# Wide two-operand work moved off GpSimd, norm gains folded into the split as columns, delta-rule state updated for two heads at once

## The chip, the cores and the metric

The kernel runs on one core of a Trainium2 chip. The metric is device time in microseconds (us) of one execution; lower is better. Engines are called PE (TensorE, matrix products), PEld (its weight loads), DVE (VectorE), ACT (ScalarE), POOL (GpSimd) and SP (SyncE, which issues the DMAs).

## The reference, cut to what matters

Two blocks run one after the other on `x` (1 x 512 x 1024, float32). The first block has two layers, and each layer is a mixer followed by a feed-forward part. The mixer projects the normed input and feeds four groups of four heads: hgrn2, gated linear attention, MLA attention and a gated delta rule. Its output norms carry a gain per head channel:

```python
def hgrn2_mixer(...):
    o = rms_norm(o, norm_g) * jax.nn.sigmoid(heads(g, HA, DV_A))     # gla and gdn: silu
def chunk_gated_delta(...):                       # per chunk of 64 tokens
    v_new = u_ - w_ @ state
    o = (q_ * exp(b_)) @ state + a_ @ v_new
    state = exp(b_last) * state + (k_ * exp(b_last - b_)).T @ v_new
```

The second block has layer A (differential attention, whose output is normed with the gain `a_subln_2` over 128 channels, times 1 - lambda_init, times a silu gate) and layer B (stick-breaking attention). Both layers also attend to a memory.

## The kernel before, in words

Everything is float32. A matrix product is three float32r products: each operand is kept as a high and a low part (`split`, `mm3`), so every weight tile of 128 x 1024 that arrives by DMA (`wr`) is cast by ACT to the high part (`wh`) and a subtraction gives the low part (`wl`) in `wload`. That subtraction runs on DVE, or on POOL where the caller gives `eng=self.G`: this is so for the tiles that `setup` preloads (two) and for those that `out_proj` preloads for the stage to come (three ahead of each feed-forward part, two ahead of layer 1 of the first block, of layer A and of layer B), 14 in all.

The program is written as generators, but its order is not theirs: `Plan` records every operation with its tiles, and `simulate` lists them by a cost model (`cost`, with a price for each engine; POOL's tensor_tensor 0.15 + 2.1 ns per element, DVE's 0.07 + 1.04 ns per element) with the program's order as the priority. The instructions are then emitted in that order, and each engine executes its own in order. The model takes the engines as independent of one another apart from data and buffers. All instructions carry one helper's line (L328), so a group in the profile is known by its tiles: `p4w`, `p4p`, `p4h` are 128 x 1024 buffers, `p` 128 x 512 ones, `st` small columns, `bc` and `cols` constants, `psA`, `psS`, `psD` PSUM banks (3, 3 and 2).

A layer of the first block runs as: norm of four token tiles (`norm_tok`, whose root comes from POOL: `rstd`), transposes and splits into `h` (`trans_split`: ACT high, DVE low), projections merged with the heads' cores (`merge`), then `out_proj` with `residual_norm` for each token tile, and interleaved with it the next norm; then 22 steps of the feed-forward part, and its `out_proj`.

What the change touches in these stages: `gate_done` (activation of a gate, then its product with the norm's gain on POOL), `finish` and `to_mixT` (product of output and gate, of the norm, transposes, split), `gla_core` (`qk`, and `AT` from the diagonal), `gdn` (three 128 x 1024 products of a mask and a column vector, `gm` twice and `sq`; `v` times beta; `kbe`; the state update of the delta rule, four operations on 64 partitions x 64 for each of 7 chunk steps), `fm_to_tm` (transposes, evacuated by ACT), `gates` and `emit_y` in layer A, and the tables `prow` (rows that become columns of `cols`) and `pbc` (rows broadcast to 128 partitions, `bc`).

Of the kernel before, what the change touches and what calls it, by code (L numbers as in the profile page):

```python
# [15 lines left out]
ALU = mybir.AluOpType  # L16
# [18 lines left out]
def shape_constants():  # L35
# [36 lines left out]
    for k, v in c.items():  # L72
# [8 lines left out]

_ROWS = [("mq", 4), ("mkv", 2), ("lb", 4), ("bgk", 2), ("hc", 6), ("f0", 66), ("g0", 24), ("pad", 20),
         ("f1", 66), ("g1", 24), ("pad2", 38)]
_BCS = [("hg", 128), ("gg", 128), ("dg", 128), ("alog", 8), ("dtb", 8), ("sub", 128), ("g16", 32)]

# [13 lines left out]
def pack(I):  # L99

    f = lambda k: np.asarray(I[k], np.float32)
    z = lambda n: np.zeros((n, 128), np.float32)
    heads = [f("a_q_norm_2")[0], f("a_k_norm_2")[0], f("mem_q_norm_2")[0], f("mem_q_norm_2")[1],
             f("mem_k_norm_2")[0], f("mem_k_norm_2")[1]]
    rows = {"mq": f("mla_q_norm_g"), "mkv": f("mla_kv_norm_g"), "lb": f("hgrn_lb_logits"), "bgk": f("gla_b_gk"),
            "hc": np.stack([np.concatenate([h, h]) for h in heads]), "pad": z(20), "pad2": z(38),
            "f0": f("ffn_conv_w")[0], "f1": f("ffn_conv_w")[1], "g0": f("gdn_conv_w")[0], "g1": f("gdn_conv_w")[1]}
    prow = np.concatenate([rows[k].reshape(-1, 128) for k, _ in _ROWS])
    bcs = {"hg": f("hgrn_norm_g"), "gg": f("gla_norm_g"), "dg": f("gdn_norm_g"), "alog": f("gdn_a_log"),
           "dtb": f("gdn_dt_bias"), "sub": f("a_subln_2"),  # L110
           "g16": np.concatenate([heads[0][:16], heads[1][:16]])}
    pbc = np.concatenate([bcs[k].reshape(-1) for k, _ in _BCS])
    w = f("w_in")
    wsm = np.concatenate([w[:, :, OFF[k]:OFF[k] + n] for k, n in (("bc", 16), ("db", 8), ("ckr", 32))], axis=2)
    return {"consts": CONST_ARR, "neg": NEG_ARR, "prow": np.ascontiguousarray(prow),
            "pbc": np.ascontiguousarray(pbc),
            "plam": np.concatenate([f(f"a_lambda_{k}_2")[0] for k in ("q1", "k1", "q2", "k2")]), "wsm": np.ascontiguousarray(wsm)}
# [496 lines left out]
class Net:  # L614
# [334 lines left out]
    def setup(self):  # L949
# [13 lines left out]
        for t in (2, 3):  # L963
            self.preload(first[t - 2], eng=self.G)
            load(t)
# [5 lines left out]
    def setup1(self):  # L971
# [16 lines left out]
        b = lambda k, l, n: bc[:, BC_OFF[k] + l * n:BC_OFF[k] + (l + 1) * n]  # L988
        self.hg, self.gg, self.dg = ([b(k, l, 64) for l in range(2)] for k in ("hg", "gg", "dg"))
        self.alog, self.dtb = ([b(k, l, 4) for l in range(2)] for k in ("alog", "dtb"))  # L990
        self.sub8, self.g16 = b("sub", 0, 128), b("g16", 0, 32)
        self.w2 = self.cst([16, 2, 128], name="w2")
# [40 lines left out]

    def to_mixT(self, o, kt0, pst):

        for g in range(2):
            ps = self.ps(pst)
            for t in range(NT):
                self.tr(ps[:, t * 128:(t + 1) * 128], o[:, t, g * 128:(g + 1) * 128])
            mt = self.p4([128, 2, S], F32R)  # L1040
            self.split(mt[:, 0, :], mt[:, 1, :], ps)
            self.mixT[kt0 + g] = mt

    def finish(self, o, gate, kt0, pst):

        sq = self.p4()
        self.act(sq, o, AF.Square)
        ss = self.st([128, 16])
        self.rsum(ss, sq.rearrange("p (a d) -> p a d", d=64))
        yield lambda: gate.get("done")  # L1050
        r = self.rstd(ss, 64)
        self.mul(o, o, gate["gate"])
        yield self.when(r)
        ov = o.rearrange("p (a d) -> p a d", d=64)
        self.mul(ov, ov, r.unsqueeze(2).broadcast_to([128, 16, 64]))
        yield self.when(o)
        self.to_mixT(o.rearrange("p (t c) -> p t c", t=NT), kt0, pst)

# [8 lines left out]
    def gate_done(self, T, f, g):  # L1067

        self.act(T["gate"], T["gate"], f)
        gv = T["gate"].rearrange("p (a d) -> p a d", d=64)  # L1070
        self.mul(gv, gv, g.unsqueeze(1).broadcast_to([128, 16, 64]), self.G)
        T["done"] = True

    def gla_core(self, q, k, b, v, dk, scale, out):
# [46 lines left out]
        qk = big()  # L1121
        self.mul(qk, q, k, self.G)
        el = self.st([128, nc8])
# [32 lines left out]
        diag = self.K["lev"][:, 6 * 64:7 * 64].unsqueeze(1).broadcast_to([128, 16, 64])  # L1156
        self.mul(a3(AT), diag, dg.unsqueeze(2).broadcast_to([128, 16, 64]), self.G)
        yield self.when(E, Q)
# [359 lines left out]

    def fm_to_tm(self, src, dst):

        dv = dst.rearrange("p (t j c) -> p t j c", t=NT, j=2)
        for j in range(2):
            ps = self.ps("D")
            for t in range(NT):
                self.tr(ps[:, t * 128:(t + 1) * 128], src[:, j * S + t * 128:j * S + (t + 1) * 128])
            self.act(dv[:, :, j, :], ps.rearrange("p (t c) -> p t c", t=NT), AF.Copy)

# [8 lines left out]
    def gdn(self, l, qkv, T0):  # L1536
# [31 lines left out]
        ex = self.st([128, 64])  # L1568
        self.act(ex, ps[:, :64], AF.Exp)
        eb, er = ex[:, 0:16], ex[:, 16:32]  # L1570
# [18 lines left out]
        m4 = lambda key: K[key].unsqueeze(1).unsqueeze(1).broadcast_to([128, 2, 8, 64])  # L1589
        self.mul(v4(gm), m4("gt64"), sta(gf), self.G)  # L1590
        yield self.when(gm)
        for half in range(2):
# [3 lines left out]
            self.act(lm[:, s], ps, AF.Exp)  # L1596
        self.mul(v4(sq), m4("gt64"), sta(nbetaf), self.G)
        yield self.when(rk)
# [46 lines left out]

        self.mul(v4(gm), m4("le64"), sta(gf), self.G)
        self.mul(v3(q), v3(q), bc16(eb))
# [12 lines left out]
        v = self.p4()  # L1660
        self.fm_to_tm(vraw, v)
        self.mul(v3(v), v3(v), bc16(betaf), self.G)
        yield self.when(Nb)
# [51 lines left out]
        self.mul(sc, betaf, eb)  # L1715
        self.mul(v3(kbe), v3(k), bc16(sc), self.G)
        self.mul(v3(k), v3(k), bc16(er))
# [19 lines left out]
        for c in range(8):  # L1737
# [11 lines left out]
            for h in range(4):  # L1749
                self.mm(ps[hr(h), (h // 2) * 64:(h // 2) * 64 + 64], kd[prs(c), tslot(h, c)], vn[prs(c), slot(h, c)])  # L1750
            for h in range(4):
                e0 = 32 + (c % 2) * 16 + (c // 2) * 4 + h
                self.stt(Sa[hr(h), c + 1, h // 2, :], Sa[hr(h), c, h // 2, :], ex[hr(h), e0:e0 + 1],
                         ps[hr(h), (h // 2) * 64:(h // 2) * 64 + 64], ALU.mult, ALU.add)
            yield self.when(Sa)
# [67 lines left out]
    def out_proj(self, W, lhs, order, done, first, second, then):  # L1823
# [26 lines left out]
        for t in range(NT):  # L1850
# [4 lines left out]
            if t == NT - 1:  # L1855
                self.preload(*then, eng=self.G)
            done(t, [ps0[t], ps1[t]])
# [267 lines left out]
    def layer_a(self, steps):  # L2125
# [114 lines left out]
        def gates(g):  # L2240
# [5 lines left out]
            def last():  # L2246
                self.act(gate[g], gate[g], AF.Silu)
                gv = gate[g].rearrange("p t (h d) -> p (t h) d", d=128)
                self.mul(gv, gv, self.sub8.unsqueeze(1).broadcast_to([128, 8, 128]), self.G)

# [45 lines left out]
    def emit_y(self, y, tag):  # L2296
# [4 lines left out]
        o = self.p4([128, 2, S], F32R, tag)  # L2301
        self.split(o[:, 0, :], o[:, 1, :], ps)
        return o
# [216 lines left out]
```

## Time and profile before

| | |
|---|---|
| time, median of 3 runs | 2048.59 us (2046.83 to 2051.95) |
| the profiled execution's own time | 2043.82 us |
| its span, first to last instruction | 2042.0 us |
| busy: PE, DVE, ACT, POOL | 1963.9, 1265.9, 955.0, 356.8 us |
| mean granted TensorE clock | 0.989 |
| DMA | 191.88 MB, mean 94 GB/s |

The span falls into six stretches: mixer of layer 0 (0 to 365 us), its feed-forward part (365 to 733), mixer of layer 1 (733 to 1089), its feed-forward part (1089 to 1457), layer A (1457 to 1750) and layer B (1750 to 2042). A profile row of a timeline gives start, length, engine, operation, tiles and shape, and in brackets how long the engine had been idle before and what ended that. A granted clock of 1.00 is the 2.4 GHz level, 0.50 the 1.2 GHz level.

### The profile page before, as it was taken

To read this page: it belongs to the slowest core of one execution; us is meant where nothing else is said; L and a number is where in the kernel's file an instruction comes from. 1 tells how busy PE (TensorE), PEld (TensorE's weight loads), DVE (VectorE), ACT (ScalarE), POOL (GpSimd) and SP (SyncE) were. 2 spreads that over 40 slices of the span, in tenths; PEclk is the share of its full clock that TensorE was granted. 3 is DMA by queue.
4 is the path that set the end of the run, shared out by engine and by line. 5 is a ranking of instruction groups with operands and counts; after the bars stand their busy time and mean duration, and the time that the engine had idled before them with its cause. 6 is when DMAs were issued, how large, how long until landed. Compare 5 with 4: busy or idle time off the path is not lost.

```text
span 2042.0 us, 33217 instructions
## 1 busy us (share of the span) xinstructions
PE 1963.9 (96%) x13254; PEld 1663.4 (81%) x13254; DVE 1265.9 (62%) x2313; ACT 955.0 (47%) x1721; POOL 356.8 (17%) x403
## 2 busy tenths in 40 slices
PE   6999999999999999999999999999999999999999
PEld 5888778888888878787788888888899988888787
DVE  7697883644442266879836444422548886558796
ACT  5763363433332246633634333322446663457782
POOL 3312121100000023112203000000323331105131
PEclk9999999999999999999999999999999999999999
DMA  5321224433332433301344333325331213331121
GB/s 159 99 71 36 71 67 164 117 100 93 94 102 93 155 108 93 76 23 55 94 150 119 93 94 102 93 93 175 114 83 49 77 62 114 126 91 53 62 73 62
DMA packets 231305, 191.88 MB, mean 94 GB/s; under 512 B 22224, under 2 KB 201072, under 8 KB 231152
## 3 DMA queue, kind: packets, MB, share of 16 engines
q1 hardware_dynamic: 231152, 189.77, 30.4%
q8 instruction: 104, 1.70, 0.4%
q14 instruction: 49, 0.40, 0.1%
HBM read 174.54 MB, written 15.20 MB: 93 GB/s over the span
## 4 chain that ended last, share of the span: by engine, by line
PE 80%; DVE 11%; ACT 3%; issue 2%; POOL 2%; DMA 1%; SPq 1%; DVEq 0%; ACTq 0%; POOLq 0%
PE psA L328 59%; PE psS L328 12%; PE psD L328 9%; DVE p4w L328 7%; DVE wl L328 1%; POOL st L328 1%; DVE p L328 1%; DVE st L328 1%; ACT p4w L328 1%; DVE p4p L328 1%; SPq L328 1%; ACT wh L328 1%; DVE p4h L328 0%; DMA p4p<-in_x_dram 0%; ACT p L328 0%
## 5 line engine op out<-in xcount | busy, mean ns | idle before, releaser
L328 PE MATMUL psA<-p4h,wh 128*128 128x512 f32 (+1 forms) x2144 | 626.0, 376 | 4.0 <-ACT p4h L328 2.6
L328 DVE TENSOR_TENSOR wl<-wr,wh 128x1024 fp32r<-128x1024 f32 (+5 forms) x290 | 336.6, 1165 | 392.2 <-ACT wh L328 386.8
L328 ACT CAST wh<-wr 128x1024 fp32r<-128x1024 f32 (+6 forms) x304 | 299.0, 990 | 474.8 <-PE psA L328 283.8
L328 PEld LDWEIGHTS psA<-p4h,wh 128*128 128x128 f32 x2144 | 392.6, 190 | 83.2 <-ACT p4h L328 4.4
L328 PE MATMUL psA<-p4h,wl 128*128 128x512 f32 (+1 forms) x1072 | 403.2, 377 | 1.5 <-DVE wl L328 1.5
L328 PE MATMUL psA<-wh,p4h 128*128 128x256 f32 (+1 forms) x1792 | 353.0, 290 | 2.1 <-DVE p4h L328 1.7
L328 PEld LDWEIGHTS psA<-wh,p4h 128*128 128x128 f32 x1792 | 284.0, 190 | 6.6 <-DVE p4h L328 2.3
L328 PE MATMUL psA<-wl,p4h 128*128 128x256 f32 (+1 forms) x896 | 259.8, 290 | 0.0
L328 POOL TENSOR_SCALAR st<-st 128x1 f32<-128x1 f32 (+4 forms) x108 | 40.0, 370 | 1139.1 <-ACT p4w L328 781.4
L328 PEld LDWEIGHTS psA<-p4h,wl 128*128 128x128 f32 x1072 | 203.9, 190 | 35.5 <-DVE wl L328 1.7
L328 PEld LDWEIGHTS psA<-wl,p4h 128*128 128x128 f32 x896 | 170.5, 190 | 1.6
L328 PE MATMUL psA<-wh,p4w 128*128 128x512 f32 (+1 forms) x540 | 159.5, 368 | 0.0
L328 ACT ACTIVATE p<-p 128x512 f32<-128x512 f32 (+2 forms) x174 | 88.1, 526 | 107.1 <-DVE p L328 105.9
L328 POOL TENSOR_TENSOR st<-st,c 128x1 f32<-128x1 f32 (+4 forms) x106 | 113.9, 1077 | 7.5
L328 PEld LDWEIGHTS psA<-wh,p4w 128*128 128x128 f32 x540 | 96.5, 188 | 18.4 <-issue 0.7
L328 ACT ACTIVATE p4w<-psA 128x256 f32<-128x256 f32 (+5 forms) x138 | 61.6, 451 | 101.9 <-PE psA L328 100.9
L328 PE MATMUL psS<-p4w,p4w 128*64 128x64 f32 (+9 forms) x800 | 98.1, 283 | 7.4 <-DVE p4w L328 7.3
L328 PE MATMUL psS<-consts,p4w 128*128 128x128 f32 (+1 forms) x448 | 71.0, 293 | 34.4 <-DVE p4w L328 18.8
L328 PE MATMUL psA<-wl,p4w 128*128 128x512 f32 (+1 forms) x270 | 98.4, 365 | 0.0
L328 PE MATMUL psS<-wh,p4w 128*128 128x512 f32 x300 | 97.4, 395 | 0.0
L328 DVE TENSOR_TENSOR p<-psA,p 128x512 f32<-128x512 f32 x54 | 37.3, 690 | 95.7 <-PE psA L328 94.2
L328 PEld LDWEIGHTS psS<-consts,p4w 128*128 128x128 f32 x448 | 55.1, 154 | 44.4 <-DVE p4w L328 17.1
(228 smaller groups left out, 3242.5 us busy)
## 6 DMA issues: line engine op xcount, KB each, us to landing
wr<-in_w_in_dram SPq DMA_DIRECT2D x44, 512.0 KB, 3.8
wr<-in_ffn_w_gate_dram SPq DMA_DIRECT2D x44, 512.0 KB, 3.8
wr<-in_ffn_w_up_dram SPq DMA_DIRECT2D x44, 512.0 KB, 3.9
wr<-in_ffn_w_down_dram SPq DMA_DIRECT2D x44, 512.0 KB, 3.5
wr<-in_w_out_dram SPq DMA_DIRECT2D x16, 512.0 KB, 4.4
wr<-in_a_w_in_dram SPq DMA_DIRECT2D x16, 512.0 KB, 3.8
wr<-in_b_w_in_dram SPq DMA_DIRECT2D x16, 512.0 KB, 3.9
p4w<-xd SPq DMA_DIRECT2D x12, 512.0 KB, 4.8
```

The costliest lines, as they stand in the source:

```text
L328: op.fn(*op.args, **op.kw)
```

## The change

No wide product or difference of two tensors is left on POOL: those that were there run on DVE, and three kinds vanish as operations of their own. The gains of the head norms (`hg`, `gg`, `dg`, `sub8`) are no rows broadcast to all partitions any more but columns, applied after the transposes, as the scale of the split in `to_mixT` and `emit_y`. The product of `v` and beta is made while the transposes are evacuated in `fm_to_tm`, by DVE in place of ACT. The delta rule's state is updated by two operations on 128 partitions in place of four on 64; for that the decay factors `ex` are laid out by halves of partitions, with three exponentials in place of one. `pbc` shrinks from 560 to 48 columns.

```diff
-            self.preload(first[t - 2], eng=self.G)
+            self.preload(first[t - 2])
...
-        self.hg, self.gg, self.dg = ([b(k, l, 64) for l in range(2)] for k in ("hg", "gg", "dg"))
+        self.hg, self.gg, self.dg = ([self.col("ng", i * 2 + l) for l in range(2)] for i in range(3))
...
-        self.sub8, self.g16 = b("sub", 0, 128), b("g16", 0, 32)
+        self.sub8, self.g16 = self.col("sub", 0), b("g16", 0, 32)
...
-            self.split(mt[:, 0, :], mt[:, 1, :], ps)
+            self.split(mt[:, 0, :], mt[:, 1, :], ps, scale=gain)
...
         self.act(T["gate"], T["gate"], f)
-        gv = T["gate"].rearrange("p (a d) -> p a d", d=64)
-        self.mul(gv, gv, g.unsqueeze(1).broadcast_to([128, 16, 64]), self.G)
-        T["done"] = True
+        T["done"], T["gain"] = True, g
...
-        self.mul(qk, q, k, self.G)
+        self.mul(qk, q, k)
...
-        self.mul(a3(AT), diag, dg.unsqueeze(2).broadcast_to([128, 16, 64]), self.G)
+        self.mul(a3(AT), diag, dg.unsqueeze(2).broadcast_to([128, 16, 64]))
...
-            self.act(dv[:, :, j, :], ps.rearrange("p (t c) -> p t c", t=NT), AF.Copy)
+            pv = ps.rearrange("p (t c) -> p t c", t=NT)
+            if scale is None:
+                self.act(dv[:, :, j, :], pv, AF.Copy)
+                continue
+            four = lambda a: a.rearrange("p t (h d) -> p t h d", h=2)
+            self.mul(four(dv[:, :, j, :]), four(pv),
+                     scale[:, :, 2 * j:2 * j + 2].unsqueeze(3).broadcast_to([128, NT, 2, 64]))
...
-        self.act(ex, ps[:, :64], AF.Exp)
+        self.act(ex[:, 0:32], ps[:, 0:32], AF.Exp)
+        for i in range(2):
+            rw = slice(i * 64, i * 64 + 64)
+            self.act(ex[rw, 32:48], ps[rw, 32:64].rearrange("p (c j s) -> p s c j", s=2, j=2)[:, i], AF.Exp)
...
-        self.mul(v4(gm), m4("gt64"), sta(gf), self.G)
+        self.mul(v4(gm), m4("gt64"), sta(gf))
...
-        self.mul(v4(sq), m4("gt64"), sta(nbetaf), self.G)
+        self.mul(v4(sq), m4("gt64"), sta(nbetaf))
...
-        self.mul(v4(gm), m4("le64"), sta(gf), self.G)
+        self.mul(v4(gm), m4("le64"), sta(gf))
...
-        self.fm_to_tm(vraw, v)
-        self.mul(v3(v), v3(v), bc16(betaf), self.G)
+        self.fm_to_tm(vraw, v, beta)
...
-        self.mul(v3(kbe), v3(k), bc16(sc), self.G)
+        self.mul(v3(kbe), v3(k), bc16(sc))
...
-            for h in range(4):
-                e0 = 32 + (c % 2) * 16 + (c // 2) * 4 + h
-                self.stt(Sa[hr(h), c + 1, h // 2, :], Sa[hr(h), c, h // 2, :], ex[hr(h), e0:e0 + 1],
-                         ps[hr(h), (h // 2) * 64:(h // 2) * 64 + 64], ALU.mult, ALU.add)
+            for j in range(2):
+                e0 = 32 + (c % 2) * 8 + (c // 2) * 2 + j
+                self.stt(Sa[:, c + 1, j, :], Sa[:, c, j, :], ex[:, e0:e0 + 1], ps[:, j * 64:j * 64 + 64], ALU.mult, ALU.add)
...
-                self.preload(*then, eng=self.G)
+                self.preload(*then)
...
                 self.act(gate[g], gate[g], AF.Silu)
-                gv = gate[g].rearrange("p t (h d) -> p (t h) d", d=128)
-                self.mul(gv, gv, self.sub8.unsqueeze(1).broadcast_to([128, 8, 128]), self.G)
...
-        self.split(o[:, 0, :], o[:, 1, :], ps)
+        self.split(o[:, 0, :], o[:, 1, :], ps, scale=self.sub8)
```

## Rows read from the trace of the kernel before

**Rows 1.** The page's first part: busy time of each engine, share of the span and instructions.

```profile
PE 1963.9 (96%) x13254; PEld 1663.4 (81%) x13254; DVE 1265.9 (62%) x2313; ACT 955.0 (47%) x1721; POOL 356.8 (17%) x403
```

**Rows 2.** Windows: a stretch, its length, busy time of PE, PEld, DVE, ACT, POOL with instructions, granted clock, DMA share, GB/s. The mixer of layer 0, its feed-forward part, the mixer of layer 1; then the two mixers without their first and last stretches.

```profile
0.00:365.00 365.00, 328.03 (x3106) 277.94 (x3106) 267.43 (x541) 188.47 (x344) 95.81 (x101) 0.99 0.31 94
365.00:733.00 368.00, 367.65 (x1664) 303.33 (x1665) 157.35 (x188) 121.10 (x168) 10.74 (x21) 0.99 0.35 108
...
38.00:300.00 262.00, 247.50 (x2647) 209.33 (x2647) 213.51 (x405) 144.66 (x255) 63.13 (x57) 0.98 0.25 71
750.00:1025.00 275.00, 258.13 (x2704) 218.25 (x2704) 217.96 (x412) 146.14 (x258) 61.77 (x51) 0.97 0.25 71
```

**Rows 3.** Windows over the eight stretches that ran at half clock: one of them, and their sum.

```profile
364.30:371.20 6.90, 6.35 (x30) 5.78 (x29) 5.89 (x10) 3.76 (x8) 3.24 (x5) 0.51 0.80 207
...
sum 44.70, PE 41.30 PEld 36.94 DVE 34.71 ACT 18.22 POOL 9.59; mean PE 5.16 PEld 4.62 DVE 4.34 ACT 2.28 POOL 1.20
```

**Rows 4.** Groups of POOL's instructions by shape, those of wide tensors with two operands: count, busy us, mean ns of one, idle before.

```profile
L328 POOL TENSOR_TENSOR wl<-wr,wh 128x1024 fp32r<-128x1024 f32 x14 | 36.8, 2634 | 38.1 <-ACT wh L328 37.8 <-POOL p4w L328 0.2
L328 POOL TENSOR_TENSOR p4w<-consts,st 128x1024 f32<-128x1024 f32 x10 | 21.4, 2149 | 7.6 <-ACT p4p L328 4.0 <-PE psS L328 3.4
L328 POOL TENSOR_TENSOR p4p<-p4p,bc 128x1024 f32<-128x1024 f32 x6 | 16.4, 2725 | 23.4 <-ACT p4p L328 23.4
L328 POOL TENSOR_TENSOR p4w<-p4w,st 128x1024 f32<-128x1024 f32 x4 | 10.6, 2645 | 89.9 <-PE psS L328 45.2 <-ACT p4w L328 44.7
L328 POOL TENSOR_TENSOR p4w<-p4w,bc 128x1024 f32<-128x1024 f32 x3 | 7.6, 2533 | 22.6 <-ACT p4w L328 22.6
L328 POOL TENSOR_TENSOR p4w<-p4p,p4p 128x1024 f32<-128x1024 f32 x2 | 5.6, 2799 | 3.8 <-ACT p4p L328 3.8
```

**Rows 5.** Groups of DVE's instructions by shape, same columns: prices of what is added or removed.

```profile
L328 DVE TENSOR_TENSOR wl<-wr,wh 128x1024 fp32r<-128x1024 f32 x258 | 320.4, 1244 | 388.8 <-ACT wh L328 383.5
L328 DVE SCALAR_TENSOR_TENSOR p4w<-p4w,st,psD 64x64 f32<-64x64 f32 x56 | 15.6, 278 | 5.4 <-PE psD L328 4.1
L328 DVE TENSOR_TENSOR p4w<-psS,p4w 128x512 fp32r<-128x512 f32 x16 | 10.4, 682 | 7.6 <-ACT p4w L328 7.6
L328 DVE SCALAR_TENSOR_TENSOR p4w<-p4w,st,psS 128x64 f32<-128x64 f32 x42 | 9.3, 272 | 0.1
L328 DVE TENSOR_TENSOR p4w<-p4w,consts 128x1024 f32<-128x1024 f32 x4 | 4.9, 1218 | 0.4 <-ACT p4w L328 0.4
L328 DVE SCALAR_TENSOR_TENSOR p4w<-psS,cols,p4w 128x512 fp32r<-128x512 f32 x6 | 4.3, 746 | 0.1
L328 DVE TENSOR_TENSOR p<-p,p4p 128x512 f32<-128x512 f32 x4 | 2.7, 687 | 1.3 <-ACT p4p L328 1.3
```

**Rows 6.** The same view, groups of DVE's with two SBUF operands whose mean is above the price of their shape.

```profile
L328 DVE TENSOR_TENSOR p4w<-p4w,st 128x1024 f32<-128x1024 f32 x14 | 22.1, 1588 | 1.4 <-POOL st L328 1.4
L328 DVE TENSOR_TENSOR p4p<-p4p,p4p 128x512 f32<-128x512 f32 x16 | 20.8, 1342 | 0.0
L328 DVE TENSOR_TENSOR p4w<-p4w,p4p 64x512 f32<-64x512 f32 x24 | 19.7, 821 | 0.2
L328 DVE TENSOR_TENSOR p4w<-p4w,p4p 128x1024 f32<-128x1024 f32 x10 | 15.3, 1530 | 2.0 <-POOL p4p L328 2.0
L328 DVE TENSOR_TENSOR p4w<-p4w,p4w 128x512 f32<-128x512 f32 x16 | 14.2, 929 | 0.0
L328 DVE TENSOR_TENSOR p4w<-p4w,p4p 128x512 f32<-128x512 f32 x12 | 12.3, 1029 | 3.5 <-ACT p4w L328 3.4
```

**Rows 7.** Timelines of DVE, POOL and PE where the mixer of layer 0 passes to its feed-forward part.

```profile
352.27 1.28 DVE L328 TENSOR_TENSOR p4p<-p4p,p4p 128x512 f32<-128x512 f32 x2
...
357.42 0.75 DVE L328 SCALAR_TENSOR_TENSOR p4p<-psA,st,p4w 128x512 f32<-128x512 f32 x1 [0.45 <-POOL st L328]
...
358.75 4.36 DVE L328 TENSOR_TENSOR p4p<-p4p,p4p 128x512 f32<-128x512 f32 x2
...
357.42 5.14 POOL L328 TENSOR_TENSOR wl<-wr,wh 128x1024 fp32r<-128x1024 f32 x2
...
363.92 0.73 PE L328 MATMUL psS<-consts,p4w 128*128 128x128 f32 x4 [3.81 <-DVE p4h L328]
```

**Rows 8.** Timeline of DVE where the second feed-forward part passes to layer A.

```profile
1460.34 4.35 DVE L328 TENSOR_TENSOR p4w<-p4w,p4w 128x512 f32<-128x512 f32 x2
```

**Rows 9.** Timelines of POOL, DVE and PE in the first 20 us.

```profile
9.39 0.19 POOL L328 TENSOR_SCALAR st<-st 128x1 f32<-128x1 f32 x1 [2.21 <-ACT p4w L328]
...
14.00 2.36 POOL L328 TENSOR_TENSOR wl<-wr,wh 128x1024 fp32r<-128x1024 f32 x1 [0.67 <-ACT wh L328]
16.32 0.57 POOL L328 TENSOR_TENSOR st<-st,c 128x1 f32<-128x1 f32 x1
...
19.12 1.94 PE L328 MATMUL psS<-consts,p4w 128*128 128x128 f32 x8 [2.14 <-DVE p4w L328]
```

**Rows 10.** Timelines of DVE and PE in the middle of layer 0's mixer.

```profile
148.27 3.70 DVE L328 TENSOR_TENSOR p4w<-p4w,p4p 128x512 f32<-128x512 f32 x3
...
154.54 0.42 PE L328 MATMUL psS<-p4w,p4w 128*64 128x64 f32 x6 [2.40 <-DVE p4w L328]
```

**Rows 11.** The chain that ended last, in order of time (start, length, what), near the end of layer 0's mixer.

```profile
290.79 2.35 POOL p4p L328
```

**Rows 12.** Timeline of DVE in layer A.

```profile
1656.67 3.37 DVE L328 TENSOR_TENSOR wl<-wr,wh 128x1024 fp32r<-128x1024 f32 x1
```

More of the change, by code (lines that the diff above doesn't have):

```diff
@@ L79 @@
 CONST_ARR, CONST_OFF, NEG_ARR = shape_constants()
-_ROWS = [("mq", 4), ("mkv", 2), ("lb", 4), ("bgk", 2), ("hc", 6), ("f0", 66), ("g0", 24), ("pad", 20),
+_ROWS = [("mq", 4), ("mkv", 2), ("lb", 4), ("bgk", 2), ("hc", 6), ("f0", 66), ("g0", 24), ("ng", 6), ("sub", 1), ("pad", 13),
          ("f1", 66), ("g1", 24), ("pad2", 38)]
-_BCS = [("hg", 128), ("gg", 128), ("dg", 128), ("alog", 8), ("dtb", 8), ("sub", 128), ("g16", 32)]
+_BCS = [("alog", 8), ("dtb", 8), ("g16", 32)]
 def _offsets(items):
@@ L105, in pack @@
     rows = {"mq": f("mla_q_norm_g"), "mkv": f("mla_kv_norm_g"), "lb": f("hgrn_lb_logits"), "bgk": f("gla_b_gk"),
-            "hc": np.stack([np.concatenate([h, h]) for h in heads]), "pad": z(20), "pad2": z(38),
+            "hc": np.stack([np.concatenate([h, h]) for h in heads]), "pad": z(13), "pad2": z(38),
+            "ng": np.concatenate([np.tile(f(k), 2) for k in ("hgrn_norm_g", "gla_norm_g", "gdn_norm_g")]), "sub": f("a_subln_2"),
             "f0": f("ffn_conv_w")[0], "f1": f("ffn_conv_w")[1], "g0": f("gdn_conv_w")[0], "g1": f("gdn_conv_w")[1]}
     prow = np.concatenate([rows[k].reshape(-1, 128) for k, _ in _ROWS])
-    bcs = {"hg": f("hgrn_norm_g"), "gg": f("gla_norm_g"), "dg": f("gdn_norm_g"), "alog": f("gdn_a_log"),
-           "dtb": f("gdn_dt_bias"), "sub": f("a_subln_2"),
+    bcs = {"alog": f("gdn_a_log"), "dtb": f("gdn_dt_bias"),
            "g16": np.concatenate([heads[0][:16], heads[1][:16]])}
@@ L1031, in setup1, with to_mixT @@
         self.ts(self.oml, self.lb, -1.0, ALU.mult, 1.0, ALU.add)
-    def to_mixT(self, o, kt0, pst):
+    def to_mixT(self, o, kt0, pst, gain):
         for g in range(2):
@@ L1056, in finish @@
         yield self.when(o)
-        self.to_mixT(o.rearrange("p (t c) -> p t c", t=NT), kt0, pst)
+        self.to_mixT(o.rearrange("p (t c) -> p t c", t=NT), kt0, pst, gate["gain"])
     def cumulate(self, b):
@@ L1517, in gdn_items, with fm_to_tm @@
                        last=lambda: self.gate_done(T, AF.Silu, self.dg[l]))]
-    def fm_to_tm(self, src, dst):
+    def fm_to_tm(self, src, dst, scale=None):
         dv = dst.rearrange("p (t j c) -> p t j c", t=NT, j=2)
```

## The prediction

> **What bounds the kernel now.** I read the page's busy times first, then windows by stage, then where the TensorE clock fell, then the timelines around PE's waits. PE is busy 1963.9 of 2042.0 us [rows 1], so at most 78 us are PE's idle time. The feed-forward parts hold none of it: 367.65 busy of 368.00 [rows 2]. The mixers hold most: in 38 to 300 us PE idles 262.0 - 247.5 = 14.5 us and in its twin, 750 to 1025, 275.0 - 258.1 = 16.9 us, while DVE is busy 213.5 and 218.0 us, some 80% [rows 2]. After a longer idle stretch PE runs at the 1.2 GHz level for a while: eight stretches, 44.7 us in sum, at a granted clock of about 0.5, with PE busy for 41.3 of them [rows 3], so about half of that, 20 us, is lost to the slow clock. What can be won at all is the idle time and those 20 us, near 100 us; the start belongs to it, where PE's second token tile comes only at 19.12 us [rows 9] and much is fixed by arriving data.
>
> Next, who makes PE wait. Where layer 0's mixer passes to its feed-forward part, PE idles 3.81 us for DVE's split of `h`; DVE was held by two adds of two SBUF operands that took 4.36 us, while the same pair takes 1.28 us one token tile earlier; beside the slow pair POOL runs two weight splits, 5.14 us from 357.42 [rows 7]. In those same microseconds DVE's operation that reads PSUM took its usual 0.75 [rows 7]. So a wide POOL operation holds up a DVE operation with two SBUF operands, and not one that takes one of them from PSUM. The same shows by groups: six groups of two-operand DVE work stand above the price of their shape (1218 ns for 1024 columns, 687 for 512 [rows 5]): 14 x 0.370 + 16 x 0.655 + 24 x 0.134 + 10 x 0.312 + 16 x 0.242 + 12 x 0.342 = 5.2 + 10.5 + 3.2 + 3.1 + 3.9 + 4.1 = 30.0 us [rows 5, 6]. The two groups of residual adds at layer boundaries (`p4p<-p4p,p4p` and `p4w<-p4w,p4w`) are 14.4 us of it, the mixers' four 15.6.
>
> The **Trainium skill**, "SBUF — State Buffer", section "Who interferes with whom", says this as a rule: an instruction of VectorE with two SBUF inputs contends with a GpSimd instruction that reads SBUF, the later one blocking fully, and one with at most one SBUF input does not. The trace agrees on both halves (4.36 against 1.28 us, 0.75 unchanged).
>
> **The change, part by part.** *Moved from POOL to DVE:* 14 weight splits, ten mask products, the wide `qk` products (two of 1024, two of half that) and two of the four `p4w<-p4w,st` products (`kbe`) [rows 4]. On DVE: 14 x 1.244 + 10 x 1.218 + 2 x 1.22 + 2 x 0.69 + 2 x 1.22 = 17.4 + 12.2 + 2.4 + 1.4 + 2.4 = 35.8 us [rows 5]. *Folded:* the other two, `v` times beta, become four evacuations from PSUM on DVE, nearest row 0.68 each, 2.7 us, in place of ACT's [rows 5]; the nine gain products vanish (16.4 + 7.6 = 24 us of POOL [rows 4]). The split with a column costs DVE 746 - 682 = 64 ns more [rows 5], 12 times in the mixers and 6 in layer A: 1.2 us; ACT's scale column I put at as much again, hidden where ACT waits. *Delta rule:* 56 operations of 278 ns become 28 of 128 partitions; the nearest row, 128x64 from PSUM, is 272 ns [rows 5]: 15.6 - 7.6 = 8.0 us less. The added exponentials are four small ACT operations, under 1 us altogether, made long before the first state step. DVE in all: 35.8 + 2.7 + 1.2 - 8.0 - 30.0 = +1.7 us; POOL loses about 100. So DVE does about the same, and 30.0 is a floor, since only six groups are counted. The gain must come from the place: a POOL operation stalls DVE by up to 2.1 us each at the spot where it happens to lie, DVE's own copy of it costs 1.24 and the planner, which takes the engines as independent, now sees it.
>
> By place:
> - *Start.* POOL computes the second tile's norm in two steps: the first at 9.39, the second only at 16.32, behind two weight splits; then DVE norms, and PE's transposes start at 19.12 after idling [rows 9]. With POOL free the root could come near 10 us, 6 us sooner; behind it wait DMA arrivals, so I take 2.5, between 0 and 5.
> - *Mixer to feed-forward, twice.* The stretch is 4.36 - 1.28 = 3.08 us; DVE's own two splits, if placed ahead of the adds, give back 2.49 [rows 5, 7]. So 0.6 to 3.1 each; 1.8 taken, 3.6 together. The half clock behind it (6.9 us [rows 3]) I leave to a rival.
> - *Feed-forward to mixer 1 and to layer A.* At A the pair of adds takes 4.35 us [rows 8], 3.1 too much, against 2.49; at layer 1 part of it. 0 to 3 each; 2.0 together.
> - *Mixers.* Added per layer: five mask products, `qk`, `kbe`, `v`: 6.1 + 1.9 + 1.2 + 1.4 = 10.6; off: the stretch 7.8, the delta rule 4.0; net about -1 of DVE. But three operations of 0.69 (2.1 us) took 3.70 us and PE idled 2.40 behind them [rows 10]; I take a fifth of the idle time, 2.9 and 3.4, together 6.3, between -3 (the net placed badly) and 14. The state step gets 0.56 us shorter, seven times a layer; its steps wait in the same queues as the rest, so I count it in DVE's load and give it nothing of its own.
> - *End of the mixers.* The chain runs through the last gain product on POOL, 2.35 us [rows 11], once a layer; it vanishes, and next late is MLA's last softmax, which ends at about the same time. Half taken: 1.2 each, 2.4; 0 to 4.7.
> - *Layer A.* A weight split of 1.24 took 3.37 us beside a gain product [rows 5, 12]; that product is gone. Of 2.1 I take 1.2.
> - *Against:* 18 column splits on both engines, some on the path: 1.0.
>
> Sum: 2.5 + 3.6 + 2.0 + 6.3 + 2.4 + 1.2 - 1.0 = 17.0 us. On the profiled execution, 2043.82 - 17.0 = 2026.8; it lies 4.8 us under the median of the runs, 2048.59, so the forecast for the median is **2031.6, say 2031**. The planner also reorders everything, since its prices differ by engine: the two mixers, one code in two orders, differ by 16.9 - 14.5 = 2.4 us of idle time [rows 2]; over four such stages that is 10 either way, hence 2021 to 2041 as the forecast's own range.
>
> **Rivals.**
> - *The relief falls into slack.* PE is 94% busy in the mixers, and stalls that no PE wait ends on are worth nothing; only the start and half of the first boundary are won: -4, **2045**. For it: DVE's total does not fall by rows. Against: PE's waits of 3.81 and 2.40 end on stretched DVE work. The Trainium skill's rule above, in its second half, points the same way: a POOL operation beside PSUM evacuations was free, and its copy on DVE is not.
> - *The clock comes back too.* If gaps of some 3 us close, the half-clock stretches behind them go: each 6.9 us is worth some 3.4, and three or four of the eight give 12; with the larger ends at the boundaries (+3): -32, **2016**.
> - *VectorE becomes the bound (slower).* In the mixers' middle DVE is 80% busy; the 10.6 - 4.0 = 6.6 us per layer come on top if the planner puts them in the in-order queue ahead of what PE waits for and the stretch was in slack: +13, and +2 x 1.2 for splits ahead of the residual adds, less 2.5 at the start: +13, **2061**. It decides from where DVE's busy share in the mixers' middle passes PE's. Against it: those same adds are stretched by more than the splits cost.
> - *The change does less than it says.* One-operand work stays on POOL; it is not in the sum.
>
> **How the numbers follow.** Forecast 0.50, slack 0.20, clock 0.17, VectorE the bound 0.13. A change under 0.3% (6.1 us) can't be told from none: faster means below 2042.4, slower above 2054.7. Faster: 0.50 + 0.17 + a fifth of the slack case = 0.71; slower 0.13; same 0.16. The range takes in forecast, slack and most of the clock case: 2010 to 2051; outside are the slower case and 0.04 below.
>
> **What would show it.** The `p4p` add group back at about 690 ns and the `p4w<-p4w,st` one at 1.22 us; PE's wait at the boundary under 2 us; the second tile's transposes well before 19 us; DVE's busy total near 1266 or lower and POOL's near 255; fewer than eight half-clock stretches if the second rival holds. The prediction is wrong if DVE's groups return to their price and PE's waits stay (slack), or if DVE's waits on PE vanish in the mixers while PE waits for DVE more (bound).

## The result, and the profile after

The changed kernel takes 2035.02 us (median of 4 runs, 2033.9 to 2038.11) against 2047.71 (4 runs, 2046.4 to 2051.95) for the kernel before in the same comparison: ratio 0.9946, 95% interval 0.9924 to 0.9968. That is 0.5% faster (0.6% by the two medians alone), 4 us above the forecast of 2031 and inside its range. The profiled execution took 2033.99 us with a span of 2032.2. The total came out nearly as forecast, but not by the forecast's sum, as the experiments show.

The page's first part, after (answers to [rows 1]):

```profile
PE 1954.1 (96%) x13254; PEld 1655.6 (81%) x13254; DVE 1250.3 (62%) x2319; ACT 946.6 (47%) x1715; POOL 265.7 (13%) x362
```

POOL lost 91 us and DVE is busy 15.6 us less, though it does more. PE's busy time fell by 9.8 us and its idle time, span less busy, stayed at 78.1; as the ends of matmuls are modelled, that split says little, and stages are compared below instead. The mixers' middles by windows, answering to [rows 2]:

```profile
38.00:300.00 262.00, 247.34 (x2663) 208.41 (x2662) 208.20 (x408) 141.38 (x255) 36.85 (x45) 0.97 0.26 71
750.00:1025.00 275.00, 259.33 (x2765) 221.39 (x2764) 212.60 (x416) 144.93 (x262) 35.69 (x39) 0.97 0.25 70
```

DVE is busy some 5 us less in each [rows 2]; PE idles 14.7 and 15.7 us there, after 14.5 and 16.9. The windows are fixed in time, and the changed kernel gets further in them (2663 and 2765 matmuls recorded, 2647 and 2704 before).

Groups of DVE's instructions by shape (count, busy us, mean ns of one, idle before), those of [rows 5, 6]:

```profile
L328 DVE TENSOR_TENSOR wl<-wr,wh 128x1024 fp32r<-128x1024 f32 x272 | 333.0, 1227 | 408.9 <-ACT wh L328 403.6
L328 DVE TENSOR_TENSOR p4w<-p4w,st 128x1024 f32<-128x1024 f32 x16 | 19.4, 1220 | 0.4 <-POOL st L328 0.2
...
L328 DVE TENSOR_TENSOR p4p<-p4p,p4p 128x512 f32<-128x512 f32 x16 | 10.2, 680 | 0.0
...
L328 DVE SCALAR_TENSOR_TENSOR p4w<-p4w,st,psD 128x64 f32<-128x64 f32 x28 | 6.6, 276 | 6.7 <-PE psD L328 6.4
```

All six stretched groups are back at the price of their shapes: `p4w<-p4w,st` at 1220 ns instead of 1588, the residual adds at 680 instead of 1342 [rows 6] (the four not shown at 683, 1217, 682 and 692); the state step costs 28 x 276 ns where 56 x 278 stood [rows 5]. So VectorE's stretch is gone. At the start the second tile's root no longer waits behind splits (POOL, then DVE's norm of that tile, then PE's transposes, answering to [rows 9]):

```profile
10.21 0.56 POOL L328 TENSOR_TENSOR st<-st,c 128x1 f32<-128x1 f32 x1
...
12.14 1.28 DVE L328 SCALAR_TENSOR_TENSOR p4w<-p4p,st,p4w 128x1024 f32<-128x1024 f32 x1
...
13.47 1.12 PE L328 MATMUL psS<-consts,p4w 128*128 128x128 f32 x4 [3.08 <-DVE p4w L328]
```

Where a layer passes to the next part, though, PE waits longer than before. Timelines (start, length, engine and instruction, idle time before it) of DVE, POOL and PE at the end of layer 0's mixer, answering to [rows 7]:

```profile
356.21 1.21 DVE L328 TENSOR_TENSOR wl<-wr,wh 128x1024 fp32r<-128x1024 f32 x1
358.15 1.30 DVE L328 SCALAR_TENSOR_TENSOR p4w<-p4p,st,p4w 128x1024 f32<-128x1024 f32 x1 [0.72 <-POOL st L328]
359.37 1.21 DVE L328 TENSOR_TENSOR wl<-wr,wh 128x1024 fp32r<-128x1024 f32 x1
361.82 1.28 DVE L328 TENSOR_TENSOR p4p<-p4p,p4p 128x512 f32<-128x512 f32 x2
...
356.24 1.24 POOL L328 TENSOR_SCALAR st<-st 128x1 f32<-128x1 f32 x1 [3.91 <-ACT p4w L328]
...
358.11 0.27 POOL L328 TENSOR_SCALAR st<-st,st 128x1 f32<-128x1 f32 x1
358.46 1.40 POOL L328 TENSOR_TENSOR st<-st,c 128x1 f32<-128x1 f32 x1
...
355.78 0.63 PE L328 MATMUL psS<-consts,p4w 128*128 128x128 f32 x4 [0.81 <-DVE p4h L328]
357.05 0.51 PE L328 MATMUL psA<-p4h,wh 128*128 128x256 f32 x2 [0.64 <-ACT p4h L328]
359.59 0.63 PE L328 MATMUL psS<-consts,p4w 128*128 128x128 f32 x4 [2.04 <-DVE p4w L328]
363.49 0.58 PE L328 MATMUL psA<-p4h,wh 128*128 128x256 f32 x1 [3.27 <-DVE p4h L328]
```

The adds take 1.28 us, not 4.36 [rows 7]. But two of the three splits stand on either side of the third token tile's norm (358.15), in front of the adds, and PE has that tile's transposes behind only two matmuls: its waits add up to 0.81 + 0.64 + 2.04 + 3.27 = 6.8 us. In the kernel before there were two waits here, 3.81 [rows 7] and 0.55 us. At the end of the first feed-forward part, in the same three timelines:

```profile
734.29 2.35 DVE L328 TENSOR_TENSOR wl<-wr,wh 128x1024 fp32r<-128x1024 f32 x2
738.36 1.28 DVE L328 SCALAR_TENSOR_TENSOR p4w<-p4w,st,p4w 128x1024 f32<-128x1024 f32 x1 [1.72 <-POOL st L328]
...
734.38 2.39 POOL L328 TENSOR_SCALAR st<-st,st 128x1 f32<-128x1 f32 x1 [3.42 <-ACT p4w L328]
...
739.79 1.08 PE L328 MATMUL psS<-consts,p4w 128*128 128x128 f32 x4 [3.65 <-DVE p4w L328]
```

POOL's one-column step, 0.27 us at 358.11 above, takes 2.39 beside DVE's two splits and ends with them; then DVE, then PE wait for it. In the kernel before, PE's longest wait there was 1.91 us (739.79).

To place gains and losses, all kernels are measured by the same long stretches of PE in the view of the chain that ended last: the start of the first projections (`psA` x168), of a late block of layer 0's mixer (`psA` x114), of the first feed-forward part (`psA` x1053), the part's last 72 matmuls, and so on. For the changed kernel the rows (start, length, engine and tile, count) are:

```profile
31.16 30.79 PE psA L328 x168
297.54 15.52 PE psA L328 x114
...
375.84 233.62 PE psA L328 x1053
710.26 16.81 PE psA L328 x72
763.78 22.23 PE psA L328 x96
...
1021.37 15.52 PE psA L328 x114
1099.56 233.64 PE psA L328 x1053
1433.98 16.80 PE psA L328 x72
```

For the kernel before they start at 34.41, 303.10, 379.29, 713.73, 762.23, 1026.84, 1103.21 and 1437.64. Differences of such starts, in us, of the profiled execution of each kernel (the other names are those of the experiments; the two feed-forward bodies, 334.1 to 334.4 each in every kernel, are left out):

| stage | before | after | p0 | p1 | p2 | y1 | y2 | c1 | b1 |
|---|---|---|---|---|---|---|---|---|---|
| start | 34.4 | 31.2 | 34.6 | 34.4 | 32.5 | 30.9 | 31.0 | 34.6 | 34.3 |
| mixer 0 | 268.7 | 266.4 | 269.5 | 264.0 | 274.4 | 268.4 | 269.5 | 271.0 | 263.8 |
| to feed-forward | 76.2 | 78.3 | 75.9 | 73.8 | 83.1 | 72.4 | 74.5 | 76.5 | 73.5 |
| feed-forward to mixer 1 | 48.5 | 53.5 | 51.7 | 47.9 | 54.5 | 47.9 | 47.9 | 50.1 | 47.9 |
| mixer 1 | 264.6 | 257.6 | 262.2 | 257.3 | 267.9 | 255.8 | 254.1 | 266.0 | 257.2 |
| to feed-forward | 76.4 | 78.2 | 75.5 | 73.9 | 80.5 | 72.0 | 73.9 | 76.8 | 73.5 |
| rest | 604.4 | 598.2 | 600.5 | 597.8 | 600.3 | 597.3 | 597.7 | 601.0 | 601.7 |

After against before: start -3.3, mixers -2.3 and -7.0, rest -6.1; to the feed-forward parts +2.1 and +1.8, feed-forward to mixer 1 +5.0; together -9.8, the difference of the spans.

### The profile page after: what moved, and what is told of

Read it like the earlier page. It is cut to its first block, busy times and chain, and to the rows that moved or that the text cites. A ratio compares the mean times of both kernels' runs of the same rounds, so it can differ in the third digit from the quotient of the medians.

```text
span 2032.2 us, 33173 instructions
## 1 busy us (share of the span) xinstructions
PE 1954.1 (96%) x13254; PEld 1655.6 (81%) x13254; DVE 1250.3 (62%) x2319; ACT 946.6 (47%) x1715; POOL 265.7 (13%) x362
## 4 chain that ended last, share of the span: by engine, by line
PE 84%; DVE 7%; ACT 3%; POOL 2%; issue 2%; DMA 1%; SPq 1%; DVEq 0%; ACTq 0%; POOLq 0%
PE psA L328 63%; PE psS L328 12%; PE psD L328 9%; DVE p4w L328 5%; POOL st L328 2%; ACT p4w L328 1%; DVE p4p L328 1%; DVE wl L328 1%; SPq L328 1%; DVE p L328 1%; ACT wh L328 0%; DMA wr<-in_w_in_dram 0%; ACT p4p L328 0%; ACT p L328 0%; DVE p4h L328 0%
## 5 line engine op out<-in xcount | busy, mean ns | idle before, releaser
L328 DVE TENSOR_TENSOR wl<-wr,wh 128x1024 fp32r<-128x1024 f32 (+6 forms) x304 | 349.0, 1152 | 413.7 <-ACT wh L328 408.4
L328 POOL TENSOR_SCALAR st<-st 128x1 f32<-128x1 f32 (+4 forms) x108 | 46.1, 427 | 1310.6 <-ACT p4w L328 908.5
L328 PEld LDWEIGHTS psS<-consts,p4w 128*128 128x128 f32 x448 | 54.5, 153 | 47.7 <-issue 19.1
```

The costliest lines, as they stand in the source:

```text
L328: op.fn(*op.args, **op.kw)
```

## The experiments

The planner orders all engines' queues by its own prices. So who executes an operation and what the planner was told can be parted: an engine object plans under one name and issues to another. Theory: the moves gain by who executes, and lose by the new order. Rivals: the columns and the delta rule make the gain; the order alone does.

**p0, p1, p2: two by two.** p0 puts the splits, mask products, `qk` and `kbe` of the changed kernel back on GpSimd:

```
-self.preload(*then)
+self.preload(*then, eng=self.G)
-self.mul(qk, q, k)
+self.mul(qk, q, k, self.G)
...
```

> The changed kernel with every operation that went from GpSimd to VectorE put back on GpSimd, for the planner too (the weight splits at the start and at the ends of the output projections, the mask products, qk and kbe). Gain columns, two heads per state operation, and v scaled in its evacuation stay. If the moves make the gain (the theory of the prediction): 2043 to 2047 us, DVE work in the mixers stretched again. If the columns and the delta rule make it: 2034 to 2037. If neither does and the gain is the planner's new order: any time in 2035 to 2052.

p1 has p0's order, p2 the changed kernel's; in the diff above `self.G` becomes `self.X`:

```
+self.X = eng("POOL", nc.vector)   # p1; in p2: eng("DVE", nc.gpsimd)
```

> The order of the run before, instruction by instruction on every engine (it was planned with these operations on GpSimd), with the same operations now executed by VectorE. Only who executes them differs from p0. If stretched DVE work is what the moves take away: 5 to 9 us below p0, near 2037, and DVE's groups at their price. If it is the planner's new order that matters: as p0 within 3 us, or slower, since DVE has 30 more operations that its queue was not planned for.

> The order of the changed kernel on every engine (planned with the moved operations on VectorE), with the same operations executed by GpSimd. If who executes them is what counts: 10 to 18 us above the changed kernel, 2045 to 2053, with stretched DVE work back. If the order counts: 2035 to 2039.

| planned as, executed by | GpSimd | VectorE |
|---|---|---|
| GpSimd's | p0 2037.46, 0.9960 (0.9946 to 0.9974) | p1 2020.99, 0.9884 (0.9871 to 0.9898) |
| VectorE's | p2 2062.68, 1.0085 (1.0071 to 1.0098) | after 2035.02, 0.9946 (0.9924 to 0.9968) |

(Medians, and ratios to the kernel before on the same chip.) Along each row only the executing engine changes: 0.76% and 1.39% of 2046, 15.5 and 28.4 us, are won. Down the right column only the order changes: 0.62%, 12.7 us, are lost. p0 by itself speaks for the rival: without the moves all but 0.14% of the gain is there. p1 shows why that is no verdict on the moves: they gain 15.5 us and their order takes nearly all of it back. p2 is slower than either expectation, and not because VectorE is stretched more: for the same work its DVE is busy 1239.6 us, p0's 1252.5, and the adds `p4p<-p4p,p4p` take 921 ns on average, in p0 1346. What p2 has beside that are waits of DVE for products that POOL makes there (who waits for whom: us in total, times, longest):

```profile
DVE p4w L328 <- POOL p4w L328: 21.4, 4, 6.0
```

p0, p1 and the changed kernel have none of these, so the 28.4 us are not the stretch alone. The 15.5 us are nearer to it: for POOL's small steps DVE's `p4w` operations wait 51.9 us in p0 and 51.2 in p1, and for a moved product or split in neither (ACT waits once for a split in p0, 2.5 us). The page's first parts of p0 and p1:

```profile
PE 1963.3 (96%) x13254; PEld 1663.9 (82%) x13254; DVE 1252.5 (61%) x2289; ACT 954.2 (47%) x1721; POOL 326.3 (16%) x392
```

```profile
PE 1949.5 (97%) x13254; PEld 1651.8 (82%) x13254; DVE 1251.3 (62%) x2319; ACT 953.9 (47%) x1721; POOL 255.1 (13%) x362
```

With 30 more operations DVE is busy 1.2 us less: what they cost, the stretch gave. p2 shows what stretch there is in the changed kernel's order; its DVE, POOL and PE where layer 0's mixer ends:

```profile
371.77 4.26 DVE L328 TENSOR_TENSOR p4p<-p4p,p4p 128x512 f32<-128x512 f32 x2
...
370.38 2.35 POOL L328 TENSOR_TENSOR wl<-wr,wh 128x1024 fp32r<-128x1024 f32 x1
373.08 2.39 POOL L328 TENSOR_TENSOR wl<-wr,wh 128x1024 fp32r<-128x1024 f32 x1 [0.35 <-ACT wh L328]
...
376.42 0.58 PE L328 MATMUL psA<-p4h,wh 128*128 128x256 f32 x1 [5.18 <-DVE p4h L328]
```

PE waits 5.18 us there, 3.27 in the changed kernel.

**x1: the next weights' splits back on GpSimd** (only `self.preload(*then, eng=self.G)`, twelve weight tiles; the planner is told GpSimd too, so the order changes with the engine).

> The changed kernel with only the weight splits at the ends of the output projections (the four next weights) put back on GpSimd. By the landmarks of the two traces, the changed kernel lost 1.7, 5.0 and 1.8 us at mixer to feed-forward, feed-forward to mixer 1 and mixer 1 to feed-forward, and won 2.2 at feed-forward to layer A; if these are the price of the splits on DVE, this run is some 6 us below the changed kernel, near 2029. If the losses come from the order or from GpSimd's small steps of the norm, it is 2033 to 2037; if the prediction's own sum at the boundaries holds (5.6 us won by the move), 2041.

2030.89 us, ratio 0.9924 (0.9910 to 0.9938): by the medians 4 us faster than the changed kernel, near the first expectation, though the intervals overlap. By the same landmarks the three passages give back 2.4, 1.7 and 2.7 us and the mixers take 2.4 and 1.3. As the change places them, these splits gain nothing on VectorE.

**y2, y1: keep VectorE, keep the old order.** y2 tells the planner GpSimd for those splits alone; y1 for the mixers' products as well, so that only the start's two splits are planned as VectorE's.

```
+self.X = eng("POOL", nc.vector)
-self.preload(*then)
+self.preload(*then, eng=self.X)
```

> The changed kernel, with the planner told GpSimd for the splits at the ends of the output projections alone; VectorE executes them as before. Theory (these splits, planned as VectorE's, are put into its queue where the norm's steps and PE's transposes are due): 14 us below the changed kernel, the 4.7, 5.6 and 4.3 us that it lost to p1 at the three layer boundaries, so 2021. Rival (the mixers' products planned on VectorE spoil the order): 2033 to 2037. Rival (only who executes matters there): as x1, 2031.

> All moved operations on VectorE, as in the changed kernel; the planner is told GpSimd for the mixers' products and for the splits at the ends of the output projections, and VectorE for the two splits at the start. Theory (the order is what the boundaries lose, the start's order is what the changed kernel wins): p1's 2021 less the 3.1 us by which the changed kernel leads it at the start, 2018. Rival (reordering is noise that one edit more rolls anew): 2022 to 2036.

y2 2018.73 (2014.2 to 2019.47), y1 2016.14 (2014.65 to 2022.02), both 0.9859 (0.9844 to 0.9874); they can't be told apart. y2 names the loss: with the same work on the same engines, the order around `then`'s splits costs 0.87% (17.8 us; 14.8 by the spans of the profiled executions). By the table 3.8 + 5.6 + 4.3 = 13.7 of it lie at the three passages. And y2 is x1's order with another executor: 0.65%, 13 us, for these splits alone. y2's timelines of PE at the first, of DVE and POOL at the second:

```profile
359.43 0.63 PE L328 MATMUL psS<-consts,p4w 128*128 128x128 f32 x4 [1.30 <-DVE p4h L328]
360.70 1.35 PE L328 MATMUL psA<-p4h,wh 128*128 128x256 f32 x3 [0.64 <-ACT p4h L328]
369.65 1.04 PE L328 MATMUL psS<-consts,p4w 128*128 128x128 f32 x8
...
733.38 1.21 DVE L328 TENSOR_TENSOR wl<-wr,wh 128x1024 fp32r<-128x1024 f32 x1
...
735.98 1.22 DVE L328 TENSOR_TENSOR wl<-wr,wh 128x1024 fp32r<-128x1024 f32 x1
...
734.48 0.19 POOL L328 TENSOR_SCALAR st<-st 128x1 f32<-128x1 f32 x1 [4.43 <-ACT p4w L328]
```

The third tile's transposes come at 369.65, 9 us of feed-forward matmuls after 360.70, and PE does not idle in front of them; the changed kernel has them behind two matmuls. At the second passage the splits no longer stand back to back, and POOL's step takes 0.19 (the next, at 735.31 and of the form that took 2.39, 0.27). y2 does not tell how much of the loss is the place of the transposes and how much that of the splits.

**z1, z3: is it the held root?** z1 lets the planner price what GpSimd's small steps take beside wide work; z3 keeps the changed kernel's order and gives the steps to ScalarE.

```
+held = 1.0 if op.kind == "tensor_scalar" and n == 1 else 0.0        # z1, in the price of POOL
-return 0.15 + (2.1e-3 if op.kind == "tensor_tensor" else 3.33e-3) * n
+return 0.15 + held + (2.1e-3 if op.kind == "tensor_tensor" else 3.33e-3) * n
...
-self.ts(ms, ss, 1.0 / n, ALU.mult, plus, ALU.add, self.G)           # z3, one column only; m0 alike
+self.X.activation(ms, ss, AF.Copy, scale=1.0 / n, bias=plus)
```

> The changed kernel; the planner counts 1.0 us more for each one-column step of the norms on GpSimd (in its trace one took 2.39 us beside two splits on VectorE, and others 1.2, where 0.2 to 0.27 is usual). Nothing else is changed. Theory (the planner takes the norm's root for earlier than it is and puts PE's transposes of the next token tile too early in PE's queue): most of the 14.6 us that the three boundaries lost comes back, 2021 to 2027. Rival (the splits' own 1.2 us in DVE's queue are the loss, wherever the transposes stand): 2033 to 2038.

> The changed kernel in its own order on every engine, with the one-column scale steps of the norms executed by ScalarE in place of GpSimd (the root itself stays on GpSimd); planned as before. Theory (VectorE's wide work with two SBUF operands holds these steps, and PE waits behind them): the 2.39 us step at feed-forward to mixer 1 and the 1.2 us ones at the other boundaries are gone, 3 to 6 us below the changed kernel, 2029 to 2032. Rival (the steps would have waited for VectorE's splits in any case): 2034 to 2036. Rival (ScalarE's queue holds them instead): 2037 or more.

z1: 2025.08, 0.9902 (0.9887 to 0.9918), the size expected, but only in part at the place: feed-forward to mixer 1 fell from 53.5 to 48.3, while the passages to the feed-forward parts kept 77.8 and 77.2 of their 78.3 and 78.2. z3: 2030.96, 0.9928 (0.9916 to 0.9941), within its expectation, but feed-forward to mixer 1 did not shorten (53.8; the mixers won 1.7 and 1.6), and its interval overlaps the changed kernel's. POOL and PE there show

```profile
734.22 2.06 POOL L328 TENSOR_TENSOR st<-st,c 128x1 f32<-128x1 f32 x2 [4.31 <-ACT st L328]
...
737.74 1.09 PE L328 MATMUL psS<-consts,p4w 128*128 128x128 f32 x4 [2.77 <-DVE p4w L328]
```

that the roots themselves are now held (two in 2.06 us; 0.55 each elsewhere). In z1 PE's next transposes come later there, with no idle time before them:

```profile
743.18 1.47 PE L328 MATMUL psS<-consts,p4w 128*128 128x128 f32 x12
```

A step of POOL in front of them still takes 1.85 us (730.91), so what came back came with the order (the two splits too stand earlier, at 727.05 and 729.03), not with a shorter step. The loss at the passages to the feed-forward parts neither run explains.

**c1, d1, b1: one part alone, on the kernel before.** c1 has the gain columns alone, d1 the state of two heads alone, b1 the moves alone in the old order (as p1).

> The kernel before with only the gains as columns of the split (nine gain products on GpSimd gone). p0 lay 8.6 us under the kernel before with columns, delta rule and v's evacuation together. If the columns make it: 2037 to 2041, with some 3.5 us of it in layer A, where nothing else of the change lies. If the delta rule makes it: 2044 to 2047.

> The kernel before with only the state of two heads per operation in the delta rule (28 operations instead of 56). If DVE's load counts by itself: 8.0 us of DVE less, 3 to 6 us faster, 2040 to 2043. If the state steps lie in slack, as the prediction took it: 2044 to 2048.

> The kernel before in its own order on every engine, with the splits, the mask products, qk, kbe and v executed by VectorE (planned as GpSimd's); gains still multiplied on GpSimd, four state operations per chunk. Theory (the moves are worth the same without the columns and the delta rule): 16.5 us below the kernel before, as p1 under p0, so 2030. Rival (the moves pay only with the gain products gone, since these go on stretching VectorE's work): 2036 to 2042.

c1 2046.54, 0.9996 (0.9986 to 1.0006): no gain. It wins 3.4 us in the rest and gives them back earlier, where the mixers end (+2.3 and +1.4) and at feed-forward to mixer 1 (+1.6). PE's waits there, in c1 and in the kernel before:

```profile
289.96 1.13 PE L328 MATMUL psS<-p4w,p4w 96*128 96x512 f32 x2 [1.14 <-DVE p4w L328]
294.46 1.08 PE L328 MATMUL psS<-consts,p4w 128*128 128x128 f32 x4 [3.31 <-DVE p4w L328]
296.47 1.73 PE L328 MATMUL psS<-consts,p4w 128*128 128x128 f32 x7 [0.93 <-DVE p4w L328]
```

```profile
292.25 0.78 PE L328 MATMUL psS<-consts,p4w 128*128 128x128 f32 x4 [2.87 <-DVE p4w L328]
293.50 1.97 PE L328 MATMUL psS<-consts,p4w 128*128 128x128 f32 x8 [0.48 <-ACT p L328]
```

The gain product is gone and the waits grew, 5.4 us against 3.4. d1 2043.06, 0.9987 (0.9978 to 0.9996), 2.7 us, just more than nothing; by the landmarks its mixers take 271.5 and 260.3 us, 2.8 more and 4.3 less, for one and the same edit in both layers, so a difference of this size in one stage can come with the order. b1 2023.63, 0.9895 (0.9881 to 0.9908): 21.5 us, more than the whole change and more than expected: the moves need neither of the other parts. That p0 gains 8 us where c1 and d1 give 0 and 2.7 is left open: `v`'s scaling in its evacuation was not tried alone, and each of these kernels has an order of its own.

**f1: y1 with z3's small steps on ScalarE.**

> y1, the fastest so far (2016), in its own order, with the norms' one-column scale steps on ScalarE, as z3 has them beside the changed kernel (4 us below it). Theory (a held step costs only where PE's next transposes stand right behind it, which y1's order avoids at the boundaries): 2014 to 2017, no more than 2 us below y1. Rival (the hold is on the path in any order): 4 us below y1, 2012 or less. Rival (ScalarE's queue): above 2018.

2014.98, 0.9849 (0.9828 to 0.9870), not to be told from y1: in an order where no transposes stand right behind the root, the held step costs nothing that can be measured. y1 and f1 are some 1.4% and 1.5% faster than the kernel before, 0.9% and 1.0% faster than the changed one.

## Why the prediction was right, and where not

- *A wide GpSimd operation holds VectorE's two-operand work: right.* With these operations gone from POOL all six groups are back at the price of their shapes. p1 differs from p0 only in who executes and is 15.5 us faster; b1 from the kernel before, 21.5. That this is the stretch is the likely reading, since DVE waits for POOL as long in p1 as in p0; no run takes the stretch away and leaves POOL's longer time for each operation. The prediction's 17.0 for everything was the size of this effect by itself, and the order took 12.7 us back: that the total came within 4 us is in part luck.
- *DVE in all +1.7 us: mis-sized, -15.6.* By the prediction's own prices for what was added and removed, 35.8 + 2.7 + 1.2 - 8.0 = 31.7, the stretch taken away comes to 31.7 + 15.6, some 47 us (an estimate); the six groups' 30.0 was called a floor.
- *Start -2.5: the size right, -3.3, the reason only in part.* The second tile's transposes start at 13.47 us, not 19.12 [rows 9]. But a free POOL alone does not do it: p1 executes the same splits on VectorE, its root is as early as the changed kernel's (10.02 and 10.21), and it wins nothing (34.4). There DVE's norm of the tile stands behind its other work, and PE's transposes start at 19.09:

```profile
10.02 0.56 POOL L328 TENSOR_TENSOR st<-st,c 128x1 f32<-128x1 f32 x1
...
17.67 4.39 DVE L328 SCALAR_TENSOR_TENSOR p4w<-p4p,st,p4w 128x1024 f32<-128x1024 f32 x3
```

  Planned as VectorE's (y1, y2, after), the splits leave the norm between them, at 12.14 in the changed kernel; p2, planned so but with the splits on POOL, still starts its projections at 32.5, 1.9 earlier than the kernel before.
- *Passages to the feed-forward parts -1.8 each, to mixer 1 and layer A -2.0 together: this is the step that failed, though not in its price.* The executor's part was as summed at the feed-forward parts, 2.1 and 1.6 by p1 against p0, and more at mixer 1, 3.8. The prediction let these splits keep their places but for "ahead of the adds"; the planner, told another price, put PE's transposes and the splits so that 13.7 us more are lost there (after against y2). Its band of 10 us "either way" for reordering was meant for this: 12.7 us came (after against p1), all on the losing side. The rival "VectorE becomes the bound" named the mechanism, splits ahead of what PE waits for, put its main price in the mixers' middle, and gave the passages 1.2 each.
- *Mixers -6.3, their ends -2.4: the sum right by mis-sized parts.* Both together measure -2.3 - 7.0 = -9.3 up to the late block. The executor alone is worth 5.5 and 4.8 (p1 against p0), the ends cost: columns alone lose 3.7 (c1), though d1's mixers differ by as much. The chain through the last gain product [rows 11] vanished as said, and in c1 PE's next wait was longer: a link of the chain that ended last was not what PE waited for.
- *Layer A -1.2 and the columns' splits +1.0: mis-sized.* The rest, which holds the passage to layer A too, won 6.1 us: 3.4 come with the columns alone (c1), 2.7 with the moves alone (b1).
- *"The clock comes back too": not in the changed kernel, but in its work.* Its half-clock stretches, summed by windows (length, then busy times), and those of b1:

```profile
sum 51.20, PE 36.56 PEld 27.91 DVE 40.53 ACT 24.33 POOL 9.50; mean PE 4.57 PEld 3.49 DVE 5.07 ACT 3.04 POOL 1.19
```

```profile
sum 23.89, PE 22.00 PEld 19.63 DVE 19.38 ACT 9.66 POOL 1.18; mean PE 4.40 PEld 3.93 DVE 3.88 ACT 1.93 POOL 0.24
```

  51.2 us, more than the 44.7 of [rows 3]: one of 6.83 us is new behind the passage to mixer 1, and those at the mixers' ends last 10.24 us, not 6.83. PE is busy in less of it, 36.6 us after 41.3, as it waits more there. In b1 the sum is 23.9. y1 came to that rival's 2016, but with 30.7 us at half clock: some 14 us less, worth about half of that (an estimate), where the rival took 12. So the number was met by luck.
- *What would have shown it.* The groups' prices, the start and DVE's total came as written; POOL's total came to 265.7, not 255, as its one-column steps took 9.4 us more than before. "PE's wait at the boundary under 2 us" did not, and that line was the warning: it failed in the changed kernel (3.27) and held in y2 (1.30). By the prediction's own sign, groups back at their price and PE's waits still there, it was wrong and the relief fell into slack. p1 speaks against slack: in p0's order the same relief came with 15.5 us.

## What to carry to other kernels

Where a planner orders the queues, moving an operation to another engine is two changes, who executes it and where everything else now stands; cost them apart, and run the old order with the new executor before judging a move. Here the relief of a stretched engine paid only where the order left room behind the steps it runs; at a passage from one layer to the next, look at how much independent work PE has queued between a norm and the transposes of its result. A link of the chain that ended last tells what was late, not what will be late when it is gone.

## What the runs showed of the hardware

The hold works in both directions, and not only between wide operations. POOL's one-column step took 2.39 us, until the second of two back-to-back splits on DVE ended, and did not get in between them; its root, 0.55 us elsewhere, took 1.40 beside one norm on DVE. The **Trainium skill**, "SBUF — State Buffer", section "Who interferes with whom", says that issue order decides who blocks. The trace agrees for the root (DVE's norm starts at 358.15, the root at 358.46) and for the first split (734.29, the step 734.38); the second split starts after the step and still went first, and why is open. The other way, in p2, a narrow step of DVE of two SBUF operands took 2.13 us beside a product on POOL, where the shape takes 0.27:

```profile
119.48 2.40 POOL L328 TENSOR_TENSOR p4w<-p4p,p4p 128x1024 f32<-128x1024 f32 x1 [34.43 <-ACT p4p L328]
...
119.88 2.13 DVE L328 TENSOR_TENSOR p4w<-p4w 128x64 f32<-128x64 f32 x1
```
